# Input projections of the recurrence and of the attention gates as seven products of quarters, with latents, gates and rope table in DRAM

## The chip, the cores and the metric

One core of a Trainium2 chip. The metric is the device time of one launch in microseconds (us), lower is better; a time shown is the median of several runs.

## The reference

Two decoder layers over 1024 tokens of width 1024. In each, one projection of the residual stream x is cut by columns into three groups: an HGRN2 recurrence of 8 heads (queries, decays, values, gates, 1024 columns each), latent attention of 8 heads (latents of 256 and 128 columns, a rotary key of 32, gates of 512), and attention into 256 memory tokens (queries and gates of 512). The gated outputs go through one output projection, a scaled residual and a LayerNorm.

```python
for l in range(DEPTH):
    h = x @ w_in[l]
    (hg_q, hg_f, hg_i, hg_gate, mla_cq, mla_ckv, mla_kr, mla_gate,
     mem_q, mem_gate) = jnp.split(h, IN_OFFSETS, axis=-1)
    y_hg = _hgrn2_group(hg_q, hg_f, hg_i, lower_bounds[l], hgrn_out_norm[l])
    y_mla = _mla_group(mla_cq, mla_ckv, mla_kr, ..., cos, sin)
    y_mem = _memory_group(mem_q, mem, w_mem_k[l], w_mem_v[l])
    y = jnp.concatenate([y_hg * silu(hg_gate), y_mla * silu(mla_gate),
                         y_mem * silu(mem_gate)], axis=-1) @ w_out[l]
    x = _layernorm(DEEPNORM_ALPHA * x + y, ln_g[l], ln_b[l])
```

The recurrence is S_t = diag(f_t) S_(t-1) + k_t v_t, o_t = S_t q_t, per head with 128 keys and 128 values. All of it is float32.

## The kernel before

The program is written in Python for a tile framework: pools (`pool`, `T`) hand out buffers by tag, a scheduler puts the instructions of each engine in an order, and each engine then executes its own list in that order and waits for semaphores. A DMA is issued from the queue of an engine (`nc.sync`: SP, `nc.scalar`: ScalarE, `nc.gpsimd`: GpSimd) and stands in that engine's list like any other instruction.

**Products.** A float32 product is made of three float32r products: both operands are split into a rounded part and the rest, and `mm3` (line 239) multiplies high by high, high by low and low by high, accumulating in PSUM. The token side x is kept transposed and split for a whole layer. A slab is 256 columns of `w_in`: `slab_aps` (line 217) loads it into a buffer `raw` (SP queue, two DMAs of 512 KB, lines 234 and 235), ScalarE casts it into `wh` (line 225) and VectorE subtracts to get `wl` (line 226), in four pieces of 512 columns; `raw`, `wh` and `wl` have two buffers each, so that one slab can be loaded and split while another is used. `proj_T` (line 244) gives a transposed result, 128 columns of weights by 1024 tokens: 48 matmuls of 128x512, hence 96 per slab. `proj_tok` (line 256) gives the values with tokens on partitions: 192 matmuls of 128x256 per slab.

**Stages.** Per layer: memory attention (`mem_attn`), the recurrence (`hgrn_group`, line 625), preparation of the latent attention (`mla_prep`, line 696), the attention itself (`mla_attend`, line 831), output product and LayerNorm (`out_group`). Layer 0 takes about 0 to 1105 us, layer 1 the rest.

**Recurrence.** Heads come in four pairs; each pair has one slab of decays F, queries Q, values V and gates G. A head is computed by a tree over the tokens of each 128-token chunk (`hg_levels`, line 525): per level ScalarE copies half of K (`xp`, line 550), TensorE does four 128x128 products (line 555), VectorE multiplies K and Q by the partial decays (lines 558, 559) and merges the result (line 564). GpSimd makes the partial decays `tot` (line 542). `hg_out` (line 569) transposes K, builds the chunk states and the outputs, `hg_fin` (line 615) applies norm and gate and writes the head to `Yd` in DRAM. Between the steps of this tree TensorE works on the products of the following slabs, which is why the order of the loop matters:

```python
lev0 = hg_levels(l, 2 * p2, F0, K0, Qs[0], AT, hp)
if p2 > 0:
    V = values(p2)
wg = slab(w_in[l], O_G + 256 * p2)
o0 = hg_out(l, 2 * p2, K0, Qs[0], AT, lev0, V, 0, hp)
G = silu_of(proj_T(wg, 0, X), hp, "G", 2)
lev1 = hg_levels(l, 2 * p2 + 1, F1, K1, Qs[1], AT, hp)
```

**Latents.** `mla_prep` projects all tokens to 416 columns (192 matmuls of 128x416), normalises (`norm`, line 733; its power on GpSimd, line 743), transposes and splits (`turn`, line 751) into `cqT` and `ckT`, and between these steps does the four gate products (`gate`, line 762). The results stay on the chip for `mla_attend`.

## Time and profile before

| | us |
|---|---|
| median of 3 runs | 2187.52 (2186.87 to 2189.01) |
| the profiled execution | 2188.02 |
| its span | 2186.2 |
| TensorE busy in it | 2139.7 (98%) |
| weight loads of TensorE | 1859.7 (85%) |
| VectorE busy | 1175.9 (54%) |
| ScalarE busy | 849.9 (39%) |
| GpSimd busy | 388.7 (18%) |

The profile comes from one execution. The span runs from its first instruction to its last; the execution's own time is 1.8 us more. The shares are averages over stages that differ. Matmuls are pipelined: the duration of one is longer than the distance from one to the next, so the pace is read from start to start in the timeline. DMA moved 72 GB/s on average.

| stage, layer 0 and 1 | about, us |
|---|---|
| memory attention | 0 to 150, 1105 to 1235 |
| recurrence | 150 to 650, 1235 to 1740 |
| latents and attention gates | 650 to 740, 1740 to 1828 |
| latent attention | 740 to 980, 1828 to 1995 |
| output, LayerNorm | 980 to 1105, 1995 to 2186 |

### The profile page before, as it was taken

The page shows a single profiled execution, that of the slowest core. Times are in us where ns is not written, and L with a number is a line of the kernel's source. Part 1 is how long each engine was busy: PE and PEld are TensorE (multiplying, and loading weights), DVE is VectorE, ACT ScalarE, POOL GpSimd, SP SyncE. Part 2 cuts the span into 40 slices and gives each one's busy share as a digit, 9 for nine tenths or more (in the row PEclk, how much of TensorE's full clock was granted, in tenths as well). Part 3 has the DMA queues.
Part 4 walks back from the last instruction along what each step waited for, and adds up shares of the span by engine and source line. Part 5 has one row for each costly group of instructions (what it writes and reads, how often), then busy time and mean ns, then how long its engine had stood idle before and what let it go on. Part 6 is the DMA issues. An engine that isn't in the chain of part 4 may idle for free.

```text
span 2186.2 us, 31364 instructions
## 1 busy us (share of the span) xinstructions
PE 2139.7 (98%) x12248; PEld 1859.7 (85%) x12248; DVE 1175.9 (54%) x2117; ACT 849.9 (39%) x1767; POOL 388.7 (18%) x577
## 2 busy tenths in 40 slices
PE   9999999999999999999999999999999999999997
PEld 7888889898989888888787888898989888888886
DVE  6530735445463678656863318354463636887524
ACT  5532222222223577534543323222232236776311
POOL 0210010101010254301112101101010103543202
PEclk9999999999999999999999999999999999999999
DMA  5411011110110100456641110111101110015322
GB/s 197 128 54 49 20 58 39 58 39 30 41 58 30 43 11 23 138 195 221 222 154 54 63 39 25 53 40 58 39 34 37 59 47 25 13 39 169 119 67 76
DMA packets 101635, 156.52 MB, mean 72 GB/s; under 512 B 6640, under 2 KB 80240, under 8 KB 101488
## 3 DMA queue, kind: packets, MB, share of 16 engines
q1 hardware_dynamic: 94128, 130.70, 18.5%
q0 software_dynamic: 4048, 13.11, 1.5%
q10 hardware_dynamic: 3312, 10.71, 1.5%
q8 instruction: 97, 1.59, 0.3%
q14 instruction: 50, 0.41, 0.1%
HBM read 129.06 MB, written 25.17 MB: 71 GB/s over the span
## 4 chain that ended last, share of the span: by engine, by line
PE 42%; DVE 3%; issue 2%; ACT 2%; POOL 1%; DMA 0%; POOLq 0%; SPq 0%; ACTq 0%; DVEq 0%
PE A L240 9%; PE A L242 9%; PE A L241 9%; PE B L555 3%; PE B L240 2%; PE B L241 2%; PE B L242 2%; PE B L902 1%; PE B L586 1%; ACT pr L888 1%; PE B L602 1%; PE B L532 1%; PE B L604 1%; PE B L926 1%; DVE nm L885 0%
## 5 line engine op out<-in xcount | busy, mean ns | idle before, releaser
L226 DVE TENSOR_TENSOR wl<-raw,wh 128x512 fp32r<-128x512 f32 (+1 forms) x360 | 237.9, 698 | 441.7 <-ACT wh L225 413.6
L240 PE MATMUL A<-x,wh 128*128 128x512 f32 x1120 | 445.6, 398 | 6.8 <-ACT x L274 5.2
L241 PE MATMUL A<-x,wh 128*128 128x512 f32 x1120 | 442.7, 395 | 0.0
L242 PE MATMUL A<-x,wl 128*128 128x512 f32 x1120 | 441.6, 394 | 0.0
L225 ACT CAST wh<-raw 128x512 fp32r<-128x512 f32 (+1 forms) x360 | 200.0, 616 | 288.6 <-PE A L241 236.7
L240 PEld LDWEIGHTS A<-x,wh 128*128 128x128 f32 x1120 | 211.6, 189 | 49.1 <-ACT x L274 5.2
L242 PEld LDWEIGHTS A<-x,wl 128*128 128x128 f32 x1120 | 211.6, 189 | 41.7
L241 PEld LDWEIGHTS A<-x,wh 128*128 128x128 f32 x1120 | 211.7, 189 | 40.2 <-DVE x L275 0.4
L240 PE MATMUL A<-wh,x 128*128 128x256 f32 (+1 forms) x576 | 169.0, 293 | 0.0
L242 PE MATMUL A<-wh,x 128*128 128x256 f32 (+1 forms) x576 | 168.9, 293 | 0.0
L241 PE MATMUL A<-wl,x 128*128 128x256 f32 (+1 forms) x576 | 168.7, 293 | 0.0
L892 POOL TENSOR_SCALAR pr<-pr,rs 128x512 f32<-128x512 f32 (+1 forms) x192 | 116.8, 618 | 144.6 <-DVE rs L889 132.9
L555 PEld LDWEIGHTS B<-Q,xp 128*128 128x128 f32 x896 | 115.6, 192 | 27.9 <-ACT xp L550 16.0
L555 PE MATMUL B<-Q,xp 128*128 128x128 f32 x896 | 133.8, 293 | 4.2 <-DVE Q L534 4.2
L275 DVE TENSOR_TENSOR pl<-B,ph 128x512 fp32r<-128x512 f32 (+1 forms) x192 | 119.7, 644 | 21.7 <-ACT ph L274 19.0
L550 ACT COPY xp<-K 128x512 f32<-128x512 f32 x112 | 71.4, 637 | 123.1 <-PE B L555 123.0
L888 ACT ACTIVATE pr<-A,nm 128x128 f32<-128x128 f32 (+7 forms) x128 | 95.6, 748 | 59.6 <-DVE nm L885 51.4
L274 ACT CAST ph<-B 128x512 fp32r<-128x512 f32 (+1 forms) x192 | 102.7, 553 | 29.9 <-PE B L902 15.3
L241 PE MATMUL A<-wl,yh 128*128 128x512 f32 x288 | 112.6, 391 | 0.7 <-DVE wl L226 0.7
L240 PE MATMUL A<-wh,yh 128*128 128x512 f32 x288 | 112.1, 392 | 0.0
L242 PE MATMUL A<-wh,yl 128*128 128x512 f32 x288 | 112.0, 390 | 0.0
L240 PEld LDWEIGHTS A<-wh,x 128*128 128x128 f32 x576 | 110.1, 191 | 0.2
(286 smaller groups left out, 4326.6 us busy)
## 6 DMA issues: line engine op xcount, KB each, us to landing
raw<-in_w_in SPq DMA_DIRECT2D x84, 512.0 KB, 4.6
raw<-in_w_out SPq DMA_DIRECT2D x32, 1024.0 KB, 4.9
Yd<-yt POOLq DMA_DIRECT2D x48, 256.0 KB, 2.3
yr<-Yd SPq DMA_DIRECT2D x28, 384.0 KB, 4.3
raw<-in_w_mk SPq DMA_DIRECT2D x8, 512.0 KB, 4.6
raw<-in_w_mv SPq DMA_DIRECT2D x8, 512.0 KB, 3.9
xr<-in_xtok ACTq DMA_DIRECT2D x8, 512.0 KB, 3.9
X1d<-xr SPq DMA_DIRECT2D x16, 256.0 KB, 2.3
```

What stands on the lines that cost most here:

```text
L225: nc.scalar.copy(h[:, s_], raw[:, s_])
L226: nc.vector.tensor_tensor(out=lo[:, s_], in0=raw[:, s_], in1=f32(h[:, s_]), op=ALU.subtract)
L240: nc.tensor.matmul(o, lhsT=lh, rhs=rh, start=first, stop=False)
L241: nc.tensor.matmul(o, lhsT=lh, rhs=rl, start=False, stop=False)
L242: nc.tensor.matmul(o, lhsT=ll, rhs=rh, start=False, stop=last)
L274: nc.scalar.copy(h, src)
L275: nc.vector.tensor_tensor(out=lo, in0=src, in1=f32(h), op=ALU.subtract)
L532: nc.tensor.matmul(dg[:, pr * P:(pr + 1) * P], lhsT=K[:, c], rhs=Q[:, c], start=True, stop=True)
L550: nc.scalar.copy(bass.AP(tensor=a.tensor, offset=a.offset, ap=[list(a.ap[0]), [n, 2], [2 * n, 256 // n], [1, n]]), half_view(K, b, 0))
L555: nc.tensor.matmul(lp[:, pr * P:(pr + 1) * P], lhsT=xp[:, pr * P:(pr + 1) * P], rhs=q_moving(Q, pr, b), start=True, stop=True)
L888: nc.scalar.activation(po, sv, AF.Exp, bias=nm, scale=1.0, accum_out=rs)
L892: nc.gpsimd.tensor_scalar(out=pr[:, c0:c1], in0=pr[:, c0:c1], scalar1=rs, scalar2=0.0, op0=ALU.mult, op1=ALU.add)
```

## The change

**Quarters.** A slab is cut into 2 x 2 quarters A(i, j): i the 128-column half, j the half of the 1024 rows; x likewise into B11, B12, B21, B22 (row half, token half). `slab_w` computes the slab's four output quarters with seven products instead of eight (Strassen's scheme in Winograd's form): four sums of weight quarters (S1, S2, S4, S3, `diff`, on GpSimd), four sums of x quarters (T1 to T4), seven `prod` of 12 matmuls of 128x512 (84 per slab), and additions of outputs: three intermediate results are copied out of PSUM by ScalarE (`keep`) and added by VectorE (`sum_into`), the others are accumulated in PSUM. Each of the seven weight operands is split by itself (512 columns). `raw` now has one buffer, `wh` and `wl` have four of a quarter each, the sums three.

**Who uses it.** All slabs of F, Q, V and G and the two slabs of the attention's gates, 18 per layer. The values now come out transposed, and 16 transposes per slab turn them. The memory attention's slabs and the latents stay as they were.

**The token sums.** `spread` makes T1 to T4 once per layer, 20 additions on GpSimd and 28 operations on VectorE (12 sums, 16 subtractions of splits), the splits' casts on ScalarE. T1 takes the place of B12.

**Order of the stages.** The latents are computed ahead of the recurrence (`latents_out`: second token half, `spread`, first token half, transposes) and written to DRAM, as are the gates, which are computed as the last two slabs of the recurrence, and the rope table. `mla_prep` loads them after the recurrence: `ckT` and `cqT` from GpSimd's queue, rope table and gates from ScalarE's. In `hg_fin` the write of `Yd` moves from GpSimd's queue to SP's. K has one buffer where it had three, and the weight pool of the other stages is closed during the recurrence.

```diff
+    def xs(X, i, kc, th):
+        return X[kc // 4][th][i][:, kc % 4]
 
...
-    def proj_tok(w, X, q):
-
-        acc = psA()
+                mm3(acc[:, sl], lh, ll, xs(X, 0, kc, hf), xs(X, 1, kc, hf), kc == 0, kc == KC - 1)
...
+    CQ = [[T(dr, [2, P, S], F32, f"CQd{l}{i}") for i in range(2)] for l in range(DEPTH)]
+    CK = [[T(dr, [P, S], F32, f"CKd{l}{i}") for i in range(2)] for l in range(DEPTH)]
+    MG = [T(dr, [4, P, S], F32, f"MGd{l}") for l in range(DEPTH)]
...
-            nc.gpsimd.dma_start(Y[hd, :, hf * 512:(hf + 1) * 512], yt)
+            nc.sync.dma_start(Y[hd, :, hf * 512:(hf + 1) * 512], yt)
...
+    def spread(l, X, hp, lp):
+        B11, B12, B21, B22 = X[0][0], X[0][1], X[1][0], X[1][1]
+        T2, T3, T4 = ([T(hp, [P, 4, 512], F32R, f"t{n}{h}", 1) for h in range(2)] for n in (2, 3, 4))
+
+        def piece():
+            return T(lp, [P, 512], F32, "t", 6)
+
+        for k in range(4):
+            raw = {}
+            for n, b, e in (("11", B11, nc.vector), ("12", B12, nc.vector), ("22", B22, nc.gpsimd), ("21", B21, nc.gpsimd)):
+                if n == "21":
+                    continue
+                raw[n] = piece()
+                e.tensor_tensor(out=raw[n], in0=f32(b[0][:, k]), in1=f32(b[1][:, k]), op=ALU.add)
+            t3 = piece()
+            nc.gpsimd.tensor_tensor(out=t3, in0=raw["22"], in1=raw["12"], op=ALU.subtract)
+            split(T3[0][:, k], T3[1][:, k], t3)
+            nc.vector.tensor_tensor(out=raw["12"], in0=raw["12"], in1=raw["11"], op=ALU.subtract)
+            nc.gpsimd.tensor_tensor(out=raw["22"], in0=raw["22"], in1=raw["12"], op=ALU.subtract)
+            split(B12[0][:, k], B12[1][:, k], raw["12"])
+            split(T2[0][:, k], T2[1][:, k], raw["22"])
+            r = piece()
+            nc.gpsimd.tensor_tensor(out=r, in0=f32(B21[0][:, k]), in1=f32(B21[1][:, k]), op=ALU.add)
+            nc.gpsimd.tensor_tensor(out=r, in0=r, in1=raw["22"], op=ALU.subtract)
+            split(T4[0][:, k], T4[1][:, k], r)
+        return dict(B11=B11, T1=B12, T2=T2, B22=B22, T3=T3, B21=B21, T4=T4)
...
     def hgrn_group(l, X):
...
+        with ExitStack() as gs_:
+            g1, sp, hp, gw = (gs_.enter_context(pool(f"{n}{l}", bufs=1, reuse_waits="tile")) for n in ("gr", "gs", "h", "gw"))
+            T(gw, [P, 48], F32, "pad")
...
+            def slab_w(c0, put, scale=(None, None)):
+
+                raw = T(g1, [P, 2048], F32, "raw", 1)
+                v = raw.rearrange("p (k c) -> p k c", k=KC)
+                s_ = w_in[l][:, c0:c0 + 256].rearrange("(k p) c -> p k c", p=P)
+                nc.sync.dma_start(v[:, 0:4], s_[:, 0:4])
+                nc.sync.dma_start(v[:, 4:8], s_[:, 4:8])
+
+                def A(i, j):
+                    return v[:, 4 * j:4 * j + 4, P * i:P * i + P]
+
+                def diff(a, b, op=ALU.subtract):
+                    t = T(g1, [P, 512], F32, "S", 3).rearrange("p (k c) -> p k c", k=4)
+                    nc.gpsimd.tensor_tensor(out=t, in0=a, in1=b, op=op)
+                    return t
+
+                acc = psA()
+                Yb, Wb = acc[:, 0:512], acc[:, 512:1024]
+
+                def prod(o, a, b, fresh):
+                    h, lo = (T(gw, [P, 512], F32R, f"w{x}", 4).rearrange("p (k c) -> p k c", k=4) for x in "hl")
+                    split(h, lo, a)
+                    kw = {} if fresh else dict(skip_group_check=True)
+                    for k in range(4):
+                        mm3(o, h[:, k], lo[:, k], X[b][0][:, k], X[b][1][:, k], fresh and k == 0, k == 3, **kw)
+
+                def keep(o, sc):
+                    t = T(sp, [P, 512], F32, "pt", 4)
+                    if sc is None:
+                        nc.scalar.copy(t, o)
+                    else:
+                        nc.scalar.activation(t, o, AF.Copy, scale=sc)
+                    return t
+
+                prod(Yb, A(0, 0), "B11", True)
+                p1 = keep(Yb, scale[0])
+                S1 = diff(A(1, 0), A(1, 1), ALU.add)
+                prod(Wb, S1, "T1", True)
+                p5 = keep(Wb, scale[1])
+                S2 = diff(S1, A(0, 0))
+                prod(Yb, S2, "T2", False)
+                u2 = keep(Yb, scale[0])
+                S4 = diff(A(0, 1), S2)
+                prod(Wb, S4, "B22", False)
+                put(0, 1, Wb, u2)
+                S3 = diff(A(0, 0), A(1, 0))
+                prod(Yb, S3, "T3", False)
+                put(1, 1, Yb, p5)
+                prod(Wb, A(0, 1), "B21", True)
+                put(0, 0, Wb, p1)
+                prod(Yb, A(1, 1), "T4", False)
+                put(1, 0, Yb, None)
+
+            def sum_into(o, src, add, sc, view=lambda t: t):
+                if add is None:
+                    if sc is None:
+                        nc.scalar.copy(o, view(src))
+                    else:
+                        nc.scalar.activation(o, view(src), AF.Copy, scale=sc)
+                elif sc is None:
+                    nc.vector.tensor_tensor(out=o, in0=view(src), in1=view(add), op=ALU.add)
+                else:
+                    for par in range(2):
+                        nc.vector.scalar_tensor_tensor(out=o[:, :, par], in0=view(src)[:, :, par], scalar=sc,
+                                                       in1=view(add)[:, :, par], op0=ALU.mult, op1=ALU.add)
+
+            def pairs(t):
+                return t.rearrange("p (c o s) -> p c o s", c=2, o=2)
+
+            def in_parity(c0, tag, scale=(None, None)):
+
+                t = [T(hp, [P, S], F32, tag, 3) for _ in range(2)]
+                slab_w(c0, lambda i, j, src, add: sum_into(by_parity(t[i], j), src, add, scale[i], pairs), scale)
...
+
+            def silu_put(tiles, then=None):
+                def put(i, j, src, add):
+                    g = tiles[i][:, j * 512:(j + 1) * 512]
+                    sum_into(g, src, add, None)
+                    t = T(sp, [P, 512], F32, "tmp", 2)
+                    nc.scalar.activation(t, g, AF.Sigmoid)
+                    nc.gpsimd.tensor_tensor(out=g, in0=g, in1=t, op=ALU.mult)
+                    if then:
+                        then(i, j, g)
+                return put
+
+            def gates(p2):
+                G = [T(hp, [P, S], F32, "G", 2) for _ in range(2)]
+                slab_w(O_G + 256 * p2, silu_put(G))
+                return G
+
+            def mla_gates(i2):
+                G = [T(hp, [P, S], F32, "G", 2) for _ in range(2)]
+                slab_w(O_MG + 256 * i2, silu_put(G, lambda i, j, g: nc.sync.dma_start(
+                    MG[l][2 * i2 + i, :, j * 512:(j + 1) * 512], g)))
+
...
+
+                def put(i, j, src, add):
+                    t = T(sp, [P, 512], F32, "tmp", 2)
+                    sum_into(t, src, add, None)
+                    pt = psB()
+                    for b in range(4):
+                        nc.tensor.transpose(pt[:, b * P:(b + 1) * P], t[:, b * P:(b + 1) * P], ident)
+                    nc.scalar.copy(V[i][:, 4 * j:4 * j + 4].rearrange("p b v -> p (b v)"), pt)
+
+                slab_w(O_V + 256 * p2, put)
                 return V
...
+            def queries(p2):
+
+                return in_parity(O_Q + 256 * p2, "Q", tuple(oml[:, l, 2 * p2 + i:2 * p2 + i + 1] if l > 0 else None
+                                                            for i in range(2)))
+
+            def levels(hd, F, Q):
+                K = T(hp, [P, S], F32, "K", 1)
+                nc.scalar.activation(K, F, AF.Sigmoid, scale=-1.0)
+                nc.scalar.activation(F, F, AF.Sigmoid)
...
-            V = values(0)
-            wf = slab(w_in[l], O_F)
-            FK = [decay(wf, 0, 0), decay(wf, 0, 1)]
+            F = in_parity(O_F, "F")
+            Q = queries(0)
             for p2 in range(4):
...
+                h0 = 2 * p2
+                K, lev = levels(h0, F[0], Q[0])
+                V = values(p2)
+                o0 = hg_out(l, h0, K, Q[0], AT, lev, V[0], hp)
+                G = gates(p2)
+                K, lev = levels(h0 + 1, F[1], Q[1])
+                hg_fin(l, h0, o0, G[0], hp)
...
+                    F = in_parity(O_F + 256 * (p2 + 1), "F")
+                else:
+                    mla_gates(0)
...
+                    for i, t in enumerate((h, lo)):
+                        nc.sync.dma_start(CQ[l][i][rc, :, s_] if si == 0 else CK[l][i][:, s_], f32(t))
+
+            w = [slab_c(0), slab_c(1)]
+            c1 = norm(1, latents(1, w))
+            ops = spread(l, X, tp, lp)
+            c0 = norm(0, latents(0, w))
+            for q, c in ((1, c1), (0, c0)):
+                for si in range(2):
+                    turn(si, q, c[si])
+            return ops
+
...
+        for i in range(2):
+            nc.gpsimd.dma_start(ckT[i], CK[l][i])
+        for i in range(2):
+            nc.gpsimd.dma_start(cqT[i], CQ[l][i].rearrange("r p t -> p r t"))
+        nc.scalar.dma_start(rtab, RT)
...
+        for i in range(4):
+            g = T(lp, [P, S], F32, "mg", 4)
+            nc.scalar.dma_start(g, MG[l][i])
+            gs.append(g)
...
+        rope_key()
+        kv = slab_aps(ld_kv, 1024)
+        k_proj(0)
+        k_odd(0)
+        return cqT, ckT, KK, gs, kv, k_proj, k_odd, rtab
...
-        X = [T(xp, [P, NB, KC, P], F32R, f"x{i}", 1) for i in range(2)]
+        X = [[[T(xp, [P, 4, 512], F32R, f"x{i}{j}{h}", 1) for h in range(2)] for j in range(2)] for i in range(2)]
...
+        tc_ = pool(f"t{l}", bufs=1, side="right", reuse_waits="tile")
+        tp = tc_.__enter__()
+        ops = latents_out(l, X, tp)
+        wps.__exit__()
+        hgrn_group(l, ops)
+        tc_.__exit__(None, None, None)
+        xc.__exit__(None, None, None)
+        wps.__enter__()
         with pool(f"l{l}", bufs=1, reuse_waits="tile") as lp:
-            prep = mla_prep(l, X, lp)
```

In the following lists a row is the line in the program (that of the kernel before or of the changed one), the operation, and what it writes and reads, with the numbers of the buffers.

SP, at the end of layer 0's recurrence, before: the last two gate slabs (`raw` from `in_w_in`), then the attention's weights.

```order
L234 DMA raw_5633<-in_w_in 128x4x256
L235 DMA raw_5633<-in_w_in 128x4x256
L768 DMA raw_5699<-in_w_uv 128x512
L769 DMA raw_5699<-in_w_uk 128x512
L833 DMA raw_5815<-in_w_uq 128x2x1024
```

The changed kernel in the same place:

```order
L671 DMA raw_5862<-in_w_in 128x4x256
L758 DMA MGd_27_94<-G_5645 128x512
L629 DMA Yd_84<-r_6017 128x512
L629 DMA Yd_84<-r_6025 128x512
L758 DMA MGd_27_94<-G_5646 128x512
...
L758 DMA MGd_27_94<-G_5861 128x512
L899 DMA raw_6094<-in_w_uv 128x512
L900 DMA raw_6094<-in_w_uk 128x512
L950 DMA raw_6124<-in_w_uq 128x2x1024
```

The attention's weights stand behind the eight writes of gates (`MGd`) and two of `Yd`.

GpSimd in the changed kernel, at the same place: L746 is the product of a gate with its sigmoid, L888 and L890 are the loads of the latents. Before, none of these stood on GpSimd here.

```order
L746 TENSOR_TENSOR G_5860<-G_5860,tmp_5943 128x512
L746 TENSOR_TENSOR G_5861<-G_5861,tmp_5966 128x512
L746 TENSOR_TENSOR G_5860<-G_5860,tmp_5987 128x512
L888 DMA ckT_1103_6043<-CKd_23_90 128x1024
L746 TENSOR_TENSOR G_5861<-G_5861,tmp_6008 128x512
L888 DMA ckT_1104_6044<-CKd_24_91 128x1024
L890 DMA cqT_1105_6045<-CQd_19_86 128x2x1024
L890 DMA cqT_1106_6046<-CQd_20_87 128x2x1024
```

One load of `ckT` has moved ahead of the last gate product, the other three loads stand behind it.

TensorE inside the recurrence of the changed kernel, at a boundary between two slabs: `t` and `x` are the token operands, `wh` and `wl` the split weights, A the accumulator.

```order
L254 MATMUL A_2836<-t_241_1673,wh_2916 128x512
L255 MATMUL A_2836<-t_240_1672,wl_2917 128x512
L253 MATMUL A_3035<-x_29_102,wh_3036 128x512
L254 MATMUL A_3035<-x_30_103,wh_3036 128x512
L255 MATMUL A_3035<-x_29_102,wl_3037 128x512
L253 MATMUL A_3035<-x_29_102,wh_3036 128x512
L253 MATMUL A_2836<-x_33_106,wh_2933 128x512
L254 MATMUL A_2836<-x_34_107,wh_2933 128x512
L255 MATMUL A_2836<-x_33_106,wl_2934 128x512
```

The next slab's first product (A_3035) begins behind the fifth product (T3) of the slab in work (A_2836), ahead of its sixth (B21). Before, a slab's products followed the other's last one.

## Rows read from the trace of the kernel before

**Rows 1.** The page: busy time of each engine, its share of the span, instructions.

```profile
PE 2139.7 (98%) x12248; PEld 1859.7 (85%) x12248; DVE 1175.9 (54%) x2117; ACT 849.9 (39%) x1767; POOL 388.7 (18%) x577
```

**Rows 2.** Windows: us, busy PE, PEld, DVE, ACT, POOL; PEclk; DMA share; GB/s.

```profile
150.00:650.00 500.00, 497.54 (x3027) 437.39 (x3026) 238.87 (x408) 137.49 (x249) 50.64 (x91) 1.00 0.13 42
```

**Rows 3.** Timeline of PE: start, duration, line, instruction; products, then transposes.

```profile
399.84 0.39 PE L240 MATMUL A<-x,wh 128*128 128x512 f32 x1
...
406.41 0.39 PE L242 MATMUL A<-x,wl 128*128 128x512 f32 x1
406.64 1.03 PE L576 MATMUL B<-idr,K 128*128 128x128 f32 x8
407.43 0.48 PE L240 MATMUL A<-x,wh 128*128 128x512 f32 x1
```

**Rows 4.** The same view: value slab at 169 us, latents at 661 us.

```profile
169.69 0.28 PE L240 MATMUL A<-wh,x 128*128 128x256 f32 x1
...
171.97 0.28 PE L241 MATMUL A<-wl,x 128*128 128x256 f32 x1
...
661.77 0.35 PE L240 MATMUL A<-wh,x 128*128 128x416 f32 x1
...
664.04 0.35 PE L240 MATMUL A<-wh,x 128*128 128x416 f32 x1
```

**Rows 5.** Timeline of DVE: one level, from L559 to the next L559.

```profile
233.05 0.69 DVE L559 TENSOR_TENSOR Q<-Q,tot 128x512 f32<-128x512 f32 x1
233.66 0.72 DVE L564 COPY_PREDICATED C<-mk,B 128x512 f32<-128x512 uint8 x1
234.28 0.68 DVE L558 TENSOR_TENSOR K<-K,tot 128x512 f32<-128x512 f32 x1
235.06 0.69 DVE L559 TENSOR_TENSOR Q<-Q,tot 128x512 f32<-128x512 f32 x1
```

**Rows 6.** Timeline of PE: the matmuls of that level.

```profile
233.89 1.13 PE L555 MATMUL B<-Q,xp 128*128 128x128 f32 x8
234.78 0.48 PE L240 MATMUL A<-x,wh 128*128 128x512 f32 x1
```

**Rows 7.** Lines, 235:640: line, engine, operation, count | busy, mean ns | idle before.

```profile
L226 DVE TENSOR_TENSOR wl<-raw,wh 128x512 fp32r<-128x512 f32 x44 | 29.5, 687 | 99.4 <-ACT wh L225 85.4 <-PE B L619 14.0
L225 ACT CAST wh<-raw 128x512 fp32r<-128x512 f32 x44 | 25.0, 632 | 65.0 <-PE A L241 65.0
L270 POOL TENSOR_TENSOR rst<-ss,mhalf 128x4 f32<-128x4 f32 x14 | 14.3, 1021 | 169.3 <-DVE ss L268 169.3
L542 POOL TENSOR_TENSOR tot<-F 128x512 f32<-128x512 f32 x7 | 7.2, 1034 | 92.1 <-ACT on L607 92.1
...
L542 POOL TENSOR_TENSOR tot<-tot 128x8 f32<-128x8 f32 x7 | 1.4, 202 | 0.5
```

**Rows 8.** Line 234, the load of a slab's first half.

```profile
DMA to landing us min/median/max: 3.3/3.8/6.3
```

**Rows 9.** Waits of PE from 235 to 290 us: total, times, longest.

```profile
PE B L555 <- DVE Q L534: 2.1, 1, 2.1
```

**Rows 10.** Windows right behind that wait, columns as in rows 2.

```profile
255.00:260.00 5.00, 3.47 (x13) 3.12 (x14) 3.17 (x5) 1.14 (x2) 0.00 (x0) 0.72 0.00 0
260.00:265.00 5.00, 5.00 (x30) 3.95 (x29) 3.30 (x6) 1.25 (x2) 0.00 (x0) 0.94 0.00 0
```

**Rows 11.** Timeline of DVE and POOL near 1100 us, LayerNorm.

```profile
1100.08 0.69 DVE L1080 TENSOR_TENSOR xr<-xr,gb 128x512 f32<-128x512 f32 x1
...
1100.99 1.30 POOL L1081 TENSOR_TENSOR xr<-xr,gb 128x512 f32<-128x512 f32 x1 [7.41 <-DMA raw<-in_w_mv]
...
1101.04 1.80 DVE L1080 TENSOR_TENSOR xr<-xr,gb 128x512 f32<-128x512 f32 x1
```

**Rows 12.** Windows with much DMA, columns as in rows 2.

```profile
10.00:20.00 10.00, 10.00 (x43) 8.23 (x42) 9.89 (x26) 8.94 (x21) 0.00 (x0) 1.00 1.05 375
980.00:1105.00 125.00, 122.64 (x599) 102.01 (x598) 94.49 (x150) 62.94 (x111) 20.91 (x17) 1.00 0.67 227
```

More of the change, by code (lines that the diff above doesn't have):

```diff
@@ L134, in constants @@
     def constants(lp):
-        cs = T(wp, [P, 2048], F32, "raw", 2)[:, 0:C_N]
+        cs = T(wpc[1], [P, 2048], F32, "raw", 2)[:, 0:C_N]
         nc.scalar.dma_start(cs, cst)
@@ L237, in slab, with mm3 @@
         return (h.rearrange("p (k c) -> p k c", k=KC), lo.rearrange("p (k c) -> p k c", k=KC))
-    def mm3(o, lh, ll, rh, rl, first, last):
-        nc.tensor.matmul(o, lhsT=lh, rhs=rh, start=first, stop=False)
-        nc.tensor.matmul(o, lhsT=lh, rhs=rl, start=False, stop=False)
-        nc.tensor.matmul(o, lhsT=ll, rhs=rh, start=False, stop=last)
+    def mm3(o, lh, ll, rh, rl, first, last, **kw):
+        nc.tensor.matmul(o, lhsT=lh, rhs=rh, start=first, stop=False, **kw)
+        nc.tensor.matmul(o, lhsT=lh, rhs=rl, start=False, stop=False, **kw)
+        nc.tensor.matmul(o, lhsT=ll, rhs=rh, start=False, stop=last, **kw)
+    def xs(X, i, kc, th):
+        return X[kc // 4][th][i][:, kc % 4]
     def proj_T(w, ci, X):
@@ L289, in mem_in @@
         for i in range(2):
-            rv = T(wp, [P, 2048], F32, "raw", 2)[:, 0:1024] if stage is None else T(stage, [P, S], F32, "p", 2)
+            rv = T(wpc[1], [P, 2048], F32, "raw", 2)[:, 0:1024] if stage is None else T(stage, [P, S], F32, "p", 2)
             rv = rv.rearrange("p (k m) -> p k m", k=4)
@@ L585, in hg_out @@
                     break
-                nc.tensor.matmul(up[:, b * P:(b + 1) * P], lhsT=kt[:, c], rhs=V[:, c, vs], start=True, stop=True)
+                nc.tensor.matmul(up[:, b * P:(b + 1) * P], lhsT=kt[:, c], rhs=V[:, c], start=True, stop=True)
             for b in range(4):
@@ new lines, in mla_prep @@
+    def mla_prep(l, lp, rp):
+        ckT = [T(rp, [P, S], F32R, f"ckT{i}", 1) for i in range(2)]
+        cqT = [T(rp, [P, 2, S], F32R, f"cqT{i}", 1) for i in range(2)]
+        KK = [[T(rp, [P, S], F32R, f"K{ab}{i}", 1) for i in range(2)] for ab in range(2)]
+        rtab = T(lp, [P, S], F32, "rtab", 1)
+        for i in range(2):
+            nc.gpsimd.dma_start(ckT[i], CK[l][i])
+        for i in range(2):
+            nc.gpsimd.dma_start(cqT[i], CQ[l][i].rearrange("r p t -> p r t"))
+        nc.scalar.dma_start(rtab, RT)
+        gs = []
+        for i in range(4):
+            g = T(lp, [P, S], F32, "mg", 4)
+            nc.scalar.dma_start(g, MG[l][i])
+            gs.append(g)
@@ L809, in rope_key, with mla_attend @@
                 split(KK[1][0][0:64, s_], KK[1][1][0:64, s_], pt[0:64])
-        wgs = [None]
-        w = [slab_c(0), slab_c(1)]
-        c0 = norm(0, latents(0, w))
-        c1 = norm(1, latents(1, w))
-        kv = None
-        for t in 'g0 t0 t1 g1 g2 kv k g3'.split():
-            if t[0] == "g":
-                gate(int(t[1]))
-            elif t == "kv":
-                kv = slab_aps(ld_kv, 1024)
-            elif t[0] == "t":
-                q = int(t[1])
-                for si in range(2):
-                    turn(si, q, (c0, c1)[q][si])
-            else:
-                rope_key()
-                k_proj(0)
-                k_odd(0)
-        return cqT, ckT, KK, gs, kv, k_proj, k_odd
-    def mla_attend(l, cqT, ckT, KK, gs, kv, k_proj, k_odd, lp, rp):
+        rope_key()
[3 more added lines that the diff above has]
+        return cqT, ckT, KK, gs, kv, k_proj, k_odd, rtab
+    def mla_attend(l, cqT, ckT, KK, gs, kv, k_proj, k_odd, rtab, lp, rp):
         def ld_q(raw):
@@ L1203, in program @@
             out_group(l, None, early)
+    wps.__exit__()
     es.close()
```

245 lines of the change are left out of this document (92 added, 153 removed).

## The prediction

> **What bounds the kernel now.** I first read the busy shares of the engines: TensorE is busy for 2139.7 of the 2186.2 us of the span, 98%, VectorE 54%, ScalarE 39%, GpSimd 18% [rows 1]. Then the windows by stage: in the recurrence of layer 0 TensorE works 497.5 of 500 us at the full granted clock, VectorE 238.9 [rows 2]. So here the time is the number of matmuls times their pace, and each matmul that goes is time won as long as TensorE gets no new wait. Third, the timeline of TensorE, for the pace: 30 products of 128x512 start between 399.84 and 406.64 us, one each 6.80 / 30 = 0.2267 us [rows 3] (the 0.39 us that a row shows is one from start to modelled end, and they overlap). The 256-column form starts 20 times from 169.69 to 171.97, each 2.28 / 19 = 0.120 us; the 416-column form of the latents 13 times from 661.77 to 664.04, each 0.189 us [rows 4]. Last, how near VectorE comes to TensorE inside the recurrence: its page share hides that one level of the state tree takes it 235.06 - 233.05 = 2.01 us without a gap [rows 5], while TensorE in the same level has 0.89 us of level matmuls (233.89 to 234.78) [rows 6] and 4 to 5 products of 0.2267 beside them, some 2.0 us. There the two engines are level.
>
> All durations are of the profiled execution, 2188.02 us with a span of 2186.2 us; the median of the three runs is 2187.52, 0.5 us less. A measurement of this kernel can tell about 0.2%, 4.4 us.
>
> **The products that go.** A slab of 256 columns is now 7 products of quarters, each 4 blocks x 3 matmuls: 84 of 128x512 instead of 96. There are 18 such slabs per layer, 36 in all. For the 28 of gates, queries and decays that is 28 x 12 x 0.2267 = 76.2 us less. A value slab was 192 x 0.120 = 23.0 us; it becomes 84 x 0.2267 = 19.0 plus 16 transposes, which run at 0.79 / 8 = 0.099 each [rows 3], 1.6: 2.4 less, and 8 x 2.4 = 19.2. Together **-95.4 us**, all on the bounding engine. That the change doesn't do this can be excluded from the order of TensorE's instructions.
>
> **What the recurrence gets in their place.** I go by a pair of heads (four slabs, 14 levels; 8 pairs in the kernel). Three things are new on TensorE's path.
>
> (a) The raw weights have one buffer instead of two. The last of a slab's seven splits needs the weight buffer that product 3 has used (four buffers), and only then is raw free: cast 0.63 and subtraction 0.69 [rows 7], landing 3.8 (3.3 to 6.3) [rows 8], again 0.63 and 0.69, in sum 6.4 us, 8.9 with the longest landing. In the order the next slab's first product stands after product 5, so 2 products, 5.44 us, cover it. TensorE stands 1.0 to 3.5 us where no level matmuls lie between two slabs, F to Q and Q to V. I take 1.3, twice: 2.6.
>
> (b) The levels. About 28 products go beside one head's seven levels. They used to bring 28 / 24 splits, now 28 / 12: 1.2 more subtractions of 0.69 on the VectorE chain that already sets the pace, and one more addition of an output quarter, also 0.69: 1.5 per head; the first level of the even head has 5 products ahead of it where it had 9 (0.9 us less cover), so 2.0 there. 3.5.
>
> (c) K has one buffer, so the next head's K must wait for the transposes of the one before: 0.5. And one wait of 2.1 us for VectorE [rows 9] was followed by a granted clock of 0.72 and then 0.94 in two slices of 5 us [rows 10], a loss of (0.28 + 0.06) x 5 = 1.7 us. If one pair in four pays that: 0.4.
>
> That is 7.0 per pair, **+56**. The ends: 1 per pair if landing and splits are always covered (8 in all), 15 if each of the four slab changes costs the 3.5 and the clock falls once per pair (about 120). I take the middle because both rows that carry it, the level rows and the landing row, are at a tie and not beyond it. The twenty 512-wide additions of GpSimd per pair (sums of weight quarters, silu products) cost nothing here while GpSimd has room: 20 x 1.30 [rows 11] of about 113 us.
>
> **The latents' place.** The latents move ahead of the recurrence, with `spread` beside them: per layer 20 additions on GpSimd, 20 x 1.30 = 26 us, and 28 on VectorE, 28 x 0.69 = 19.3 us. The recurrence's second product needs T1, its third T2, and its memory the buffers of the latents. TensorE has only 192 x 0.189 = 36.3 us of latents and 12 transposes (1.2) to fill. If the two engines exclude each other, spread ends 4.5 + 45.3 = 49.8 us after the latents begin (4.5: landing 3.8 and a first subtraction), and the norm and turning of the second half follow on VectorE, some 4.5 (power 1.02 [rows 7], five operations of 0.69): 54.3, and TensorE stands 16.8. If they run side by side, 26 + 4.5 + 4.5 = 35 lies under the 37.5, and about 1 us (the power) is left. The nearest row is one of both engines at work: an addition of VectorE that took 0.69 alone took 1.80 while GpSimd's ran, 1.11 of GpSimd's 1.30 [rows 11]. That is nearer to exclusion; since some of spread, which reads only x, can go ahead of the latents, I take 11. Two layers: **+22**, ends 2 and 33.
>
> **Between recurrence and attention.** Before, four gate products (48 matmuls each) and the latents stood here and covered every load. Now the order puts key and query projections right behind the last product of the recurrence, at E. Their inputs come from DRAM: ckT 1 MB and cqT 2 MB in GpSimd's queue, rope table 0.5 and gates 2 in ScalarE's, weights 1.5 in SP's, 7.0 MB by shape. The last silu product of GpSimd (L746) stands ahead of ckT's second load and of cqT, so they are issued no sooner than E + 0.63 + 0.63 + 1.30 = E + 2.5. In SP's queue the attention's weights stand behind the eight gate writes. The fastest stretch of the trace moved 375 GB/s, the output stage 227 [rows 12]: all but the last half MB goes beside or ahead of cqT, and 6.5 MB at 375 are 17.3 us, so cqT is there at E + 19.8. TensorE has 8 transposes and 6 products, 2.2 us, until then: idle 17.6. If GpSimd's queue alone had the bandwidth (2.5 MB after ckT's first load): 7; at 227 GB/s for all: 29. I take 18 since all queues are filled at the same moment and nothing orders them. Two layers: **+36**, ends 14 and 58.
>
> **The sum.** 2188.0 - 95.4 + 56 + 22 + 36 = 2206.6; less the 0.5 to the median about 2206, said as 2207. With all low ends 2188.0 - 95.4 + 8 + 2 + 14 = 2117, with all high ones 2304.
>
> **The rivals.**
>
> R1, the cover holds in the recurrence (faster). In the order new products stand between level matmuls wherever old ones did; the 2.0 us tie becomes harmless if the splits are done early. Then 1 us per pair is left: 2188.0 - 95.4 + 8 + 22 + 36 = 2158.6. It decides from (95.4 - 58 - 4.4) / 8 = 4.1 us per pair: below that the kernel is measurably faster. For it speaks that over 500 us of the recurrence TensorE lost only 2.5 us [rows 2], although VectorE was level with it then too; against it the single raw buffer and the doubled splits.
>
> R2, VectorE and GpSimd get in each other's way in the recurrence (slower still). The rows of [rows 11] show one addition held for the length of the other engine's. Per pair VectorE has 62 operations with two operands in SBUF (28 of levels, 28 subtractions, 6 others), and GpSimd is busy for 20 x 1.30 + 2 x 3.0 (seven groups of `tot`, 1034 to 202 ns, 20.9 us in 7 heads [rows 7]) + 4 x 1.02 = 36 of 113 us, 0.32. Each hit costs half of a GpSimd operation, 0.65: 62 x 0.32 x 0.65 = 12.9 us of VectorE per pair. About half stands in the levels, on TensorE's path: 6 more per pair, 13 x 8 = 104, and 2188.0 - 95.4 + 104 + 22 + 36 = 2255. Against it: with `tot` alone on GpSimd the level rows show 0.68 to 0.72 [rows 5]. The Trainium skill, "SBUF — State Buffer", section "Who interferes with whom", has it as a rule that a VectorE instruction with two SBUF inputs and a GpSimd instruction that reads SBUF shut each other out; the trace agrees in that one place, 1.80 for 0.69, and it is this rule that speaks against the change.
>
> R3, gain and waits cancel within 4.4 us: the same sum with 3 to 4.7 per pair.
>
> **How the numbers follow.** The forecast has 0.40, R1 0.36, R2 0.16, R3 0.08. The forecast's own range, with 5 to 11 per pair, is 2192 to 2240. R1 reaches from 2117 to 2182, and a quarter of it lies under 2135; of R2 a third lies above 2285. Left out are 0.25 x 0.36 + 0.3 x 0.16, about 0.14, and with a little for what I haven't seen the range is 2135 to 2285. Faster by over 0.2%: R1, 0.36. Within: 0.08. Slower: forecast and R2, 0.56.
>
> **What would show it.** TensorE's busy time of products must fall by the pace, and the granted clock in the recurrence stay near 1.00 but for short dips. (a) is right if TensorE's waits list a first product of a slab behind ScalarE's cast or VectorE's subtraction of the raw weights, 1 to 2 us each, 16 times; (b) if level matmuls wait for VectorE; the latents' term if one gap of about 11 us per layer ends on a T buffer or on a turned latent; the last term if in each layer a wait of 15 to 20 us ends on the DMA of cqT or ckT. R1 is right if recurrence windows show TensorE above 98% and 113 us per pair or less; R2 if VectorE's additions have means well above 0.69 beside GpSimd. I am wrong at the root if the pace of a product is not 0.2267 any more, or if a stage that the change doesn't touch (memory attention, output) moves by more than a few us.

## The result and the profile after

The changed kernel takes 2344.4 us (2342.6 to 2345.0), the one before 2187.6 in the same comparison: **1.0715 times as long, interval 1.0696 to 1.0733**. The forecast was 2207, the range 2135 to 2285: the sign was right, the size far off. The profiled execution has a span of 2342.8 us, 156.6 more than before.

The page of the changed kernel, busy time of each engine, beside [rows 1]:

```profile
PE 2112.8 (90%) x11176; PEld 1758.1 (75%) x11176; DVE 1422.5 (61%) x2353; ACT 997.1 (43%) x1987; POOL 710.2 (30%) x784
```

TensorE has 1072 matmuls less and is busy 26.9 us less, but it now stands 230 us of the span (46.5 before). Windows of 500 us in the recurrence of layer 0 and of layer 1, columns as in [rows 2]:

```profile
220.00:720.00 500.00, 452.39 (x2374) 363.55 (x2372) 306.15 (x456) 184.64 (x312) 156.82 (x150) 1.00 0.13 41
1385.00:1885.00 500.00, 447.20 (x2321) 359.94 (x2321) 293.88 (x462) 180.41 (x304) 148.09 (x147) 0.99 0.13 41
```

Where [rows 2] had 497.5 of 500 there are now 452 and 447, at a granted clock of 1.00 and 0.99. TensorE's waits over the whole span, total, times, longest:

```profile
PE B L253 <- ACT wh L238: 37.5, 4, 16.0
PE A L253 <- ACT pt L694: 27.4, 33, 1.1
PE B L625 <- DVE r L617: 22.7, 13, 3.6
PE A L253 <- DVE G L725: 21.6, 24, 1.5
PE B L769 <- DVE tmp L725: 17.2, 16, 1.3
PE B L864 <- DVE kr L856: 14.3, 1, 14.3
PE B L864 <- ACT pr L853: 14.3, 1, 14.3
PE B L561 <- DVE Q L565: 8.8, 16, 1.2
PE A L253 <- ACT pt L696: 8.7, 9, 1.2
PE A L253 <- DVE F L725: 4.3, 5, 0.9
PE A L253 <- DVE Q L728: 4.2, 4, 1.0
PE A L253 <- DVE Q L725: 3.4, 4, 0.9
```

The first row (start of the attention) and the two of L864 (latents) stand where waits were forecast. The six rows of L253 on accumulator A are not in the prediction at all: a product waits for the copy (`keep`, L694 and L696) or the addition (`sum_into`, L725 and L728) that reads A. They come to 69.6 us in 79 waits, none of them longer than 1.5. By the order of the operands, all 79 stand where a slab goes on in its own accumulator, none at a slab's first product. The timeline of one of them, TensorE and then ScalarE:

```profile
222.17 0.39 PE L255 MATMUL A<-t,wl 128*128 128x512 f32 x1
223.53 0.50 PE L253 MATMUL A<-x,wh 128*128 128x512 f32 x1 [0.97 <-ACT pt L694]
223.86 0.40 PE L254 MATMUL A<-x,wh 128*128 128x512 f32 x1
...
222.37 0.62 ACT L279 CAST wh<-raw 128x512 fp32r<-128x512 f32 x1 [2.88 <-PE A L254]
222.90 0.58 ACT L694 COPY pt<-A 128x512 f32<-128x512 f32 x1
```

The third product ends at 222.56; its copy starts behind a cast that the same end released, and the fourth product starts when the copy is done, though it writes the other half. The listed wait is 0.97; counted from the start due at 222.17 + 0.2267 it is 1.13, and the next start comes 0.1 late: 1.24 us for this handover. Over a pair of heads (from one pair's first diagonal matmul, L538, to the next one's) the step is 127.8 us in layer 0 and 131.5 in layer 1 (means of three), against 121.5 before. Three slabs of a pair lose 12 products each at 0.2267 and the value slab 2.4 us, 10.6 in all (the attention's four gate slabs, 10.9 of the 95.4 us, lie outside the steps), so products alone would have made it 110.9. So 18.7 us per pair were lost on the mean, where 7 were forecast.

### The profile page after: what moved, and what is told of

It is laid out like the page before. It is cut to its first block, busy times and chain, and to the rows that moved or that the text cites. A ratio compares the mean times of both kernels' runs of the same rounds, so it can differ in the third digit from the quotient of the medians.

```text
span 2342.8 us, 30451 instructions
## 1 busy us (share of the span) xinstructions
PE 2112.8 (90%) x11176; PEld 1758.1 (75%) x11176; DVE 1422.5 (61%) x2353; ACT 997.1 (43%) x1987; POOL 710.2 (30%) x784
## 3 DMA queue, kind: packets, MB, share of 16 engines
q1 hardware_dynamic: 104656, 150.10, 19.4%
## 5 line engine op out<-in xcount | busy, mean ns | idle before, releaser
L253 PE MATMUL A<-x,wh 128*128 128x512 f32 x800 | 332.9, 418 | 43.7 <-ACT pt L694 23.0
L254 PE MATMUL A<-x,wh 128*128 128x512 f32 x800 | 320.1, 400 | 0.0
L255 PE MATMUL A<-x,wl 128*128 128x512 f32 x800 | 318.0, 399 | 0.0
L253 PEld LDWEIGHTS A<-x,wh 128*128 128x128 f32 x800 | 153.5, 192 | 92.6 <-ACT pt L694 34.3
L253 PE MATMUL A<-t,wh 128*128 128x512 f32 x432 | 181.3, 420 | 33.4 <-DVE G L725 13.1
L279 ACT CAST wh<-raw 128x512 fp32r<-128x512 f32 (+1 forms) x124 | 72.8, 591 | 291.4 <-PE A L254 150.9
L239 DVE TENSOR_TENSOR wl<-raw,wh 128x512 fp32r<-128x512 f32 (+2 forms) x216 | 142.2, 703 | 88.8 <-ACT wh L238 88.6
L280 DVE TENSOR_TENSOR wl<-S,wh 128x512 fp32r<-128x512 f32 x144 | 123.3, 859 | 84.7 <-ACT wh L279 84.4
L255 PE MATMUL A<-t,wl 128*128 128x512 f32 x432 | 171.2, 396 | 0.0
L254 PE MATMUL A<-t,wh 128*128 128x512 f32 x432 | 170.6, 395 | 0.0
L238 ACT CAST wh<-raw 128x512 fp32r<-128x512 f32 (+2 forms) x216 | 118.2, 606 | 100.3 <-PE A L254 43.6
L280 DVE TENSOR_TENSOR wl<-raw,wh 128x512 fp32r<-128x512 f32 (+1 forms) x124 | 83.9, 681 | 103.9 <-ACT wh L279 101.7
L561 PE MATMUL B<-Q,r 128*128 128x128 f32 x896 | 132.7, 292 | 10.7 <-DVE Q L565 8.8
L253 PEld LDWEIGHTS A<-t,wh 128*128 128x128 f32 x432 | 82.0, 190 | 65.0 <-DVE G L725 17.4
L746 POOL TENSOR_TENSOR G<-G,tmp 128x512 f32<-128x512 f32 x48 | 68.3, 1423 | 182.7 <-ACT tmp L745 182.7
```

Of the source, the lines that this page charges most:

```text
L238: nc.scalar.copy(h[:, s_], raw[:, s_])
L239: nc.vector.tensor_tensor(out=lo[:, s_], in0=raw[:, s_], in1=f32(h[:, s_]), op=ALU.subtract)
L253: nc.tensor.matmul(o, lhsT=lh, rhs=rh, start=first, stop=False, **kw)
L254: nc.tensor.matmul(o, lhsT=lh, rhs=rl, start=False, stop=False, **kw)
L255: nc.tensor.matmul(o, lhsT=ll, rhs=rh, start=False, stop=last, **kw)
L279: nc.scalar.copy(h, src)
```

## The experiments

Unless said otherwise an edit starts from the changed kernel (2344.4), and "step" is the distance from pair to pair.

**e1: two accumulators.** The accumulators' pool is reopened for the recurrence with two tags.

```diff
-                acc = psA()
-                Yb, Wb = acc[:, 0:512], acc[:, 512:1024]
+                Yb, Wb = (T(py, [P, 512], F32, t, 2) for t in "YW")
```

> The two halves of a slab's accumulator become two tiles of their own (Y and W), so that a product is not made to wait for the copy of the other half. Theory H (handover: each product waits until ScalarE or VectorE has read the result of the product before it, 79 listed waits of 69.6 us, and some 0.16 us more for each start after a wait): the waits on line 694, 696 and 725 fall to under a third, and the time falls by 65 to 95 us against the changed kernel, to 2250 to 2280. Rival Q (the readers are late in their queues, the shared tile only names the wait): the waits come back on the same reads two products later, the time falls by less than 25 us, to 2320 or more.

2238.3 us (1.0233 of before, 1.0217 to 1.0248): 106 less. The waits of TensorE now:

```profile
PE B L263 <- ACT wh L248: 35.6, 4, 15.4
PE B L874 <- DVE kr L866: 29.3, 2, 14.9
PE B L571 <- DVE Q L550: 28.7, 12, 3.3
PE B L602 <- ACT tk L593: 5.5, 3, 2.2
PE Y L263 <- DVE G L735: 4.8, 3, 1.8
PE W L263 <- DVE G L735: 4.5, 2, 3.0
```

Theory H holds, and the gain is larger than it said: the 17 us of waits of the values' transposes (L769) and the 22.7 behind `hg_fin` (L625), which stood in the same queues, are gone too, but the first level of a head now waits 28.7. Nothing came back two products later, as rival Q has it. The step is 117.1 and 117.2 us, 6.2 above 110.9. That the two halves were one tile was the cause of what the recurrence lost beyond the forecast (6.2 per pair are left, 7.0 were forecast): no instruction was added or taken away.

**e2: no weight sums.** `diff` returns its first operand.

```diff
-                    t = T(g1, [P, 512], F32, "S", 3).rearrange("p (k c) -> p k c", k=4)
-                    nc.gpsimd.tensor_tensor(out=t, in0=a, in1=b, op=op)
-                    return t
+                    return a
```

> The four sums of weight quarters on GpSimd are left out: the products S1, S2, S3, S4 take a plain quarter instead (their values are not the reference's). GpSimd loses 144 additions and VectorE its subtractions beside them. Theory H: TensorE waits for accumulators and not for the sums, so the time falls by 0 to 20 us, to 2324 to 2344, with VectorE's subtraction back from 0.86 to about 0.69 us. Rival L (the lock of VectorE and GpSimd sets the pace of the recurrence, 6 us per pair by the prediction): it falls by 45 us or more, to under 2300.

2327.4, 17 less: inside theory H's range. But this total hides two movements. The step fell to 123.6 and 128.5 us, 3.6 per pair, and from the first head's diagonal to the last gate product the two layers became 40 us shorter; VectorE was busy 4.5 us less per pair, and the subtraction took 0.71. The start of the recurrence became 22 us longer, for the most part by a wait that is new:

```profile
PE A L253 <- ACT wh L279: 16.8, 2, 8.7
```

ScalarE now does the first slab's casts behind its last work on the latents, where they stood between before. So the total is theory H's, but rival L is not out: where the handover stands, GpSimd's sums cost up to 40 us in the recurrence, near the 45 that rival L asked for. The run takes the sums away as a whole and doesn't tell the engines' exclusion from the wait for a sum.

**e3: token sums on VectorE.** In `spread`, `nc.gpsimd` becomes `nc.vector`, 20 times.

> The 20 GpSimd operations of the token sums go to VectorE, the rest stays. Theory L (the two engines exclude each other there, the 14.3 us gap per layer is the lock): VectorE has 48 operations of 0.69 and no lock, the gap falls from 14.3 to 2 to 8 us per layer, the slow clock behind it gets shorter, and the time falls by 15 to 35 us, to 2309 to 2329. Rival V (VectorE's own length decides): 20 x 0.69 = 13.8 us more on VectorE, the gap stays or grows to 28 us, the time is 2344 to 2375.

2330.1, 14.3 less. The gap at the latents fell from 28.6 us to 12.4 in both layers together, although VectorE had 20 operations more: theory L. The subtractions of T1's split, 1.78 us in the median before, took 0.68. The time lies just short of theory L's range: the clock gave nothing back on top of the gap's 16.2.

**e4: gate loads late.** The four loads of gates move to SP's queue, behind `w_uq`.

```diff
-            nc.scalar.dma_start(g, MG[l][i])
+            nc.sync.dma_start(g, MG[l][i])
```

> The four loads of the attention's gates go from ScalarE's queue to SP's, behind the attention's weights. Theory A (ScalarE stands 10.1 us on these loads and they take 2 of 7 MB ahead of the weights): the casts of K come 8 to 10 us earlier, the weights 3 to 6 us, and the gap of 14.9 + 3.5 us per layer falls to 8 to 13; with the clock behind it the time falls by 10 to 25 us, to 2319 to 2334. Rival B (the DMA engines are full at 380 to 407 GB/s and the weights land when they land): the casts come earlier but TensorE's gap falls by less than 2 us per layer, the time stays at 2339 to 2346.

2335.2, 9.2 less, between the two theories, and the wait on L238 fell from 37.5 to 28.4, by a quarter. ScalarE's casts of the weights in layer 0, changed kernel and e4:

```profile
792.73 0.71 ACT L238 CAST wh<-raw 128x256 fp32r<-128x256 f32 x2 [1.09 <-DMA raw<-in_w_uv]
801.26 2.18 ACT L238 CAST wh<-raw 128x512 fp32r<-128x512 f32 x4 [5.46 <-DMA raw<-in_w_uq]
```

```profile
788.94 0.71 ACT L238 CAST wh<-raw 128x256 fp32r<-128x256 f32 x2 [9.54 <-DMA raw<-in_w_uv]
796.09 0.62 ACT L238 CAST wh<-raw 128x512 fp32r<-128x512 f32 x1 [1.09 <-DMA raw<-in_w_uq]
```

In both the casts wait for the weights to land. In e4 ScalarE is free and stands 9.54 us for them, so its blocked queue was not what set this end. The weights land 2.6 and 4.0 us earlier (4.1 and 5.0 in layer 1), counted from the last gate product, now that the 2 MB of gates no longer go ahead of them: that is the second half of theory A.

**e5: gate products on VectorE**, on e1: `nc.gpsimd.tensor_tensor(out=g, in0=g, in1=t, op=ALU.mult)` becomes `nc.vector`.

> On top of the two accumulators (2238): the 48 products of a gate with its sigmoid go from GpSimd to VectorE. There the first level of a head waits 28.7 us in all (12 waits) for the product Q x F of VectorE, which takes 2.28 us for 1.21 where a gate product of GpSimd (2.95 for two) runs beside it. Theory L (the lock of the two engines makes that wait): Q x F is back at 1.2 us, the waits fall below 16 us, the time by 8 to 20 us, to 2218 to 2230. Rival V (VectorE's own load makes it): 48 x 0.69 = 33 us more on VectorE, the waits stay or grow, the time is 2238 to 2262.

2213.6, 24.7 less than e1, more than theory L said. VectorE and GpSimd in e1, and line L550 there and in e5 (duration min/median/max):

```profile
427.38 2.28 DVE L550 TENSOR_TENSOR Q<-Q,F 128x1024 f32<-128x1024 f32 x1
...
425.64 2.95 POOL L756 TENSOR_TENSOR G<-G,tmp 128x512 f32<-128x512 f32 x2
...
L550 DVE TENSOR_TENSOR Q<-Q,F x16: 1198/1744/2290, 252.8 to 1779.8; 128x1024 f32<-128x1024 f32 x16
```

```profile
L550 DVE TENSOR_TENSOR Q<-Q,F x16: 1195/1204/1210, 252.2 to 1764.3; 128x1024 f32<-128x1024 f32 x16
```

Q x F is held while GpSimd multiplies a gate, up to 1.1 us; without that all 16 take 1.20. The Trainium skill, "SBUF — State Buffer", section "Who interferes with whom", states this rule, and these rows agree. The wait for Q x F fell only from 28.7 to 19.8, though, above the 16 expected, and the step from 117.2 to 115.8; about 10 us more came where nobody looked, at the start of the attention. GpSimd's queue no longer holds the loads of the latents behind gate products: in layer 0 the first load of `ckT` is issued at 698.8 us and not at 728.4. The wait on the casts of `wh` fell from 35.6 to 13.5, those on G and `kb` (the rope key, before TensorE turns it) rose from 13.8 to 25.9.

**e6: token sums last**, on e1, with e4's edit: `spread` wholly on VectorE and called behind `norm` and `turn`.

```diff
-            ops = spread(l, X, tp, lp)
             c0 = norm(0, latents(0, w))
...
-            return ops
+            return spread(l, X, tp, lp)
```

> On top of the two accumulators (2238): the token sums are written behind the norm and the turning of the latents and wholly on VectorE, and the gates' loads stand behind the attention's weights (as in the fourth run, 9 us). Theory N (the norm of the second half stands behind the sums in VectorE's and ScalarE's order, and TensorE stands 14.6 us per layer for it, with the slow clock behind): this gap falls to under 5 us per layer, TensorE's clock stays up, and the time falls by 35 to 50 us, to 2188 to 2203. Rival T (VectorE's 33 us of sums and 8 of norm are longer than TensorE's 38 us of latents wherever they stand): the wait comes back at the products with T1 to T4, 6 to 12 us per layer, and the time falls by 18 to 30 us only, to 2208 to 2220.

2208.6, 29.7 less. The gap went as theory N says, from 29.3 to 9.9 us, and no wait on a T operand came in its place, so rival T's mechanism is out; but the time is rival T's: the gap (19.4 us less) and the casts of the weights (22.9 for 35.6) give about the 29.7, and the clock that theory N priced on top gave nothing. The windows of e1 behind the gap, and of e6:

```profile
205.00:210.00 5.00, 3.90 (x18) 3.74 (x19) 3.99 (x11) 3.52 (x8) 3.72 (x3) 0.50 0.21 81
210.00:215.00 5.00, 5.00 (x26) 4.29 (x25) 4.49 (x7) 3.45 (x7) 2.22 (x3) 0.92 0.78 299
```

```profile
195.00:200.00 5.00, 3.28 (x15) 3.13 (x16) 3.13 (x10) 3.81 (x9) 4.34 (x4) 0.66 0.13 50
200.00:205.00 5.00, 4.78 (x27) 3.81 (x26) 5.00 (x9) 2.79 (x6) 2.10 (x3) 1.00 0.71 272
```

In e1, after a gap of 14 us, the granted clock is 0.50 (the lower level, 1.2 GHz) in the slice in which work begins. What TensorE does there are transposes beside the norms; that they have little to lose is likely, not shown.

**e7: Q x F first**, on e6 with e5's edit: Q x F is written ahead of the two masked copies of the diagonal.

> On top of e6 (2208.6): the gates' products go to VectorE as in e5, and in each head Q x F is done ahead of the two masked copies of the diagonal, which no level needs. Theory C (the chain diagonal matmuls, two copies of 0.73, Q x F, first level is what TensorE waits for: 30.2 us in 13 waits): 15 to 22 us from the gates and 8 to 15 more from the order; the waits on Q x F fall under 10 us and the time to 2172 to 2186. Rival V (VectorE is the pace of the whole level stretch, what is moved ahead is paid back behind it): only the gates' part, 2187 to 2194, and new waits of the levels on the merges.

2192.4, 16 less: rival V's range. The step is 115.7, as in e5 (115.8), so the new order gave nothing that shows beyond the gates' part. The waits on Q x F fell from 30.2 to 24.6, not under 10 (e5 had 19.8). The order came about only in part: in all 16 heads one masked copy still stands ahead of Q x F in VectorE's list, and in every second head subtractions and a gate product too. So theory C was not put to its test, and rival V's mechanism is not shown.

**e8: latents loaded early**, on e7: `ckT` and `cqT` in the left pool, the second pair of gate tiles under the tags Q and F.

> On top of e7: the tiles for the loaded latents lie in memory that is free after the last head and not only after the last product, so that their loads can start some 20 us earlier; the second pair of gate tiles no longer waits for the writes of the first. Theory M (memory that the last product still reads holds the loads back): TensorE's gap at the start of the attention (9.5 + 2.5 us in e6, 8.4 + 2.6 in the second layer, and 1.8 to 3 behind gate tiles) falls to 3 to 7 us per layer; 12 to 24 us less than e7. Rival W (the attention's weights decide, which stand behind the eight gate writes in SP's queue): the latents are there early and the gap still ends on the weights, 0 to 8 us less than e7.

2194.6, no less (the profiled execution took 2201.4). The edit did the opposite of what it was for. GpSimd's queue in layer 0, e7 and e8:

```profile
689.75 1.19 POOL L899 DMA_DIRECT2D ckT<-CKd  x2 [4.55 <-PE Y L265]
```

```profile
715.28 1.19 POOL L899 DMA_DIRECT2D ckT<-CKd  x2 [30.15 <-PE B L944]
```

The loads of `ckT` are issued 25.5 us later and not some 20 earlier, since GpSimd's queue now stands 30 us until the rope key's transposes (L944) are done. TensorE waits for `kb` (14.3 us) and for the DMA of `ckT` (15.1) and `cqT` (6.0). Neither theory M nor rival W was put to its test.

**e9: gate writes on GpSimd's queue**, on e7, with e8's gate tiles.

> On top of e7 (2192.4): the second pair of gate tiles takes free buffers of Q and F, and the eight gate writes go from SP's queue to GpSimd's, so that the attention's weights stand behind no write of a gate. Theory W (weights behind the gate writes, and gate tiles behind their own writes: 10.6 us of waits on G, 7.1 on the weights' cast in e7): both waits go, 10 to 18 us less than e7, 2174 to 2183. Rival P (the loads of cqT stand behind the writes in GpSimd's queue instead, and their 2 MB land 6 to 8 us after the last product): a wait on cqT of 3 to 8 us per layer takes the place, 2185 to 2194.

2193.8: rival P's time (the profiled execution took 2199.6). The waits on G for the second accumulator are gone (10.6 before; 3.6 for the first are left). In their place `kb` rose from 8.7 to 14.3 and the weights' cast from 7.1 to 8.7, and waits for the DMA of `cqT` came up (5.2 in all, less than rival P's 3 to 8 per layer). The first load of `ckT` is issued at 707.7, 18 us later than in e7, behind the gate writes. e7 to e9 show one gap that is filled from three queues: when one comes earlier, another sets the end.

**e10: a product as cover**, on e9: the next slab's first product is written between Q x F and the levels.

> On top of e9: the next slab's first product is written ahead of the levels of each head, so that 12 products stand between the diagonal's matmuls and the first level where 8 stood (0.9 us more cover, 16 heads). Theory C (the first level waits 24.6 us in all for VectorE's Q x F, for want of cover): the waits fall by 10 to 15 us and the time by 8 to 15. Rival V (the cover only moves the products: VectorE is the pace of the stretch, the levels behind are short of products): the waits move to the later levels or to K's transposes and the time falls by less than 4 us.

2175.0 us, 18.8 less than e9 and 0.9945 of before (0.9933 to 0.9957). The wait on Q x F fell from 23.2 to 9.2 us, the step from 116.1 to 113.5. Theory C, with 5 us more than the waits show and 4 more than its range; the granted clock over the steps rose from 0.99 to 1.00, which may be the rest.

**e11: loads in order**, on e10: the rope table behind the weights in SP's queue, the gates behind `cqT` in GpSimd's.

> On top of e10 (2175.0): the rope table's load goes from ScalarE's queue, where it waits from 701 to 711 us for a gate write and holds the casts of the attention's weights, to SP's behind the weights, and the gates' loads stand behind those of cqT in GpSimd's queue. Theory S (ScalarE standing on a load, and 2 MB of gates beside cqT, make the second part of the gap: waits of 6.5 and 4.0 us in layer 0, 4.1 and 4.3 in layer 1): both go, 10 to 20 us less, 2155 to 2165. Rival D (the 3 MB of latents need that long after the last product in any order): the wait moves to cqT, 0 to 6 us less, 2169 to 2175.

2165.1 us, 9.9 less, just short of theory S's range: **0.9901 of before (0.9884 to 0.9917)**. ScalarE's wait for a gate write, 10.45 us in e10's layer 0, is gone. This version is faster than both kernels, by little but outside the interval. It still waits on `kb` for 14.5 us, the largest row that is left.

## Why the prediction was wrong

**The products.** Right in count and pace. 84 matmuls per slab replaced 96 or 192, and where products follow each other they start 0.22 to 0.23 us apart as in [rows 3]. TensorE's busy time, named as the sign, fell by only 26.9 us (63.3 in e1, 73.0 in e11): it also counts 0.39 to 0.50 us for a product that no other follows closely, and stretches at the lower clock. That all 95.4 us were there to be had follows from count and pace; the best run, e11, is 22.5 us faster than before.

**The recurrence: the step that failed.** "Three things are new on TensorE's path" left out the fourth and largest: after each of the seven products somebody reads the accumulator, and both halves are one tile, so the next product waits for that read. Priced: nothing. Measured: 18.7 us lost per pair against 7.0, 150 for 56, above even the high end of 120. The view that held it was the changed program itself: `Yb, Wb = acc[:, 0:512], acc[:, 512:1024]` stands in the diff, and I took the copies for work beside the path. A second sentence failed with it: that GpSimd's sums "cost nothing here". While the products waited for their readers, the weight sums cost 3.6 per pair (e2). With the tile split (e1) the loss is 6.2 per pair, so the other three terms came out near in sum, by luck in part, since they did not one by one. (a) The single raw buffer, 2.6: no wait on it is listed in the recurrence; 0. (b) The levels, 3.5: 28.7 / 8 = 3.6 in e1, all at the first level of a head, for Q x F, and in part through GpSimd's gate products. (c) K's single buffer and the clock, 0.9: no wait on K is listed; `tk`, the copy of the turned K (5.5 in e1), is 0.7 per pair. The other 1.9 is in no large row; the granted clock over the steps of e1 was 0.99 and 0.98, where it was 1.00 before.

**The latents.** Forecast 11 per layer, gap 14.3: the right mechanism (the norm of the second half stands behind the token sums, e6, and VectorE's and GpSimd's parts of these hold each other up, e3), and a size between the row that I named as nearest (16.8) and the 11 that I took.

**The start of the attention.** Forecast 18 per layer, waits 37.5 in the two: right in size, and right in that all loads go at the same moment (about 400 GB/s from 785 us until the weights landed at 801 in layer 0). Wrong was which load ends it: TensorE waits for the attention's weights, behind the gate writes and beside the gates' loads (e4), not for `cqT` or `ckT`. What lies outside the steps of the pairs took 252 - 150 = 102 us (252 is the 156.6 of the span and the 95.4 of the products), 44 more than the 58 forecast for the two stages. The listed waits of 28.6 and 37.5 are in it, the handovers of the attention's four gate slabs, and a granted clock of 0.92 and 0.94 between the latents and the first head and of 0.70 and 0.62 ahead of the attention; no run separated the rest.

**The rivals.** R1 was out in this form; e10 and e11 come near what it described, with 113.5 per step, 2.6 above the products alone where R1 has 1, and TensorE at 98% from the first head to the last gate product. R2's lock is real, at a lower price: without the weight sums VectorE was busy 4.5 us less per pair, where R2 had 12.9 for all of GpSimd's work, and the step was 3.6 shorter. After the tile split, e5 gave 25, about half of it by the steps and most of the rest through the order of one queue.

## What to carry to other kernels

When a sum of products is made in pieces that are read in between, give each piece an accumulator tile of its own, and read the order of the built program at the boundary of two products before costing anything else. A wait of one microsecond looks harmless until it recurs 80 times; price what follows each new reader of an old tile. A total can hide two movements, as in e2, and an edit of the order has to be looked up in the built program before it counts as a test (e7, e8). And a change that saves matmuls on a bounding engine needs its cover rebuilt: here the same arithmetic went from 7% slower to 1% faster by tiles, by order and by which engine does the additions.

## What the runs showed of the hardware

In the handover shown, a start after a wait cost TensorE more than the wait that the list shows: 1.24 us for 0.97. The exclusion of VectorE and GpSimd fell unevenly: the subtraction of a summed weight quarter took 0.86 us on average beside GpSimd's sums (0.71 without them), Q x F up to 2.29 for 1.20. And in the windows shown beside e6, with gaps of about 5 us at the latents, the clock stood at 0.66 in one slice and at 1.00 in the next; in e1, with gaps of 14 us, at 0.50 and 0.92 in the two slices behind. Shortening these gaps gave back their length and no more: 14.3 us of time for 16.2 us of gap in e3.
